# Rotary tables copied on chip, late constants, and products by pieces of tokens, in the start-up of a hybrid decoder block

## The chip, the cores and the metric

The kernel runs on all 8 cores of one Trainium2 chip (two dies: cores 0 to 3 and 4 to 7). The time is the device time of the slowest core, in microseconds (us). Most executions agree within 0.3%. Some fall in a slow state, in which the cores of a die run at a lower granted clock and the time is several per cent longer. Ratios of two kernels are computed as the mean time of one kernel's fast runs over that of the other's fast runs of the same rounds on the same chip, so they are not quite the ratio of the medians that are quoted.

In the profile PE is TensorE's matmuls, PEld its weight loads, DVE is VectorE, ACT ScalarE, POOL GpSimd and SP SyncE. SPq is SyncE as the issuer of transfers.

## The reference, cut to what matters

The whole program is one decoder block: a gated short convolution and a latent attention side by side, then a feed-forward network. The change touches only the first stage, in which every core computes the key/value latents of all 4096 tokens.

```python
def rope_tables(positions, dtype):
    inv_freq = ROPE_THETA ** (-jnp.arange(0, QK_ROPE_DIM, 2, dtype=jnp.float32) / QK_ROPE_DIM)
    ang = positions.astype(jnp.float32)[..., None] * inv_freq          # (B, S, 32)
    cos = jnp.cos(ang)[:, :, None, :].astype(dtype)
    sin = jnp.sin(ang)[:, :, None, :].astype(dtype)
    return cos, sin

# ... in reference():
u = rmsnorm(h, ln1_g[l])
z = u @ w_in[l]
zb, zc, zv, q_lat, kv_lat, k_rope, gates = jnp.split(z, IN_SPLIT_IDX, axis=-1)
# ... kv_lat (512 columns) and k_rope (64 columns) are needed for all tokens;
#     k_rope gets the rotary embedding from cos and sin
```

## The kernel before

Tokens come in 16 groups of two blocks of 128 tokens (so 256 columns in a product). For each group TensorE multiplies 16 slices of the input weights (128 rows each) with the tokens, in five column tiles m = 0 to 4: 80 products of 128x256. A slice of weights is loaded as float32 and scaled by ScalarE with the norm's gain into bfloat16 before it can be used; group 0's products follow those 16 scalings one by one.

Three loads:

- the *tokens* of a group, loaded and converted to bfloat16 by transfers that GpSimd issues (`xpiece`), two of 512 KB for a group;
- the *own blocks*, one float32 copy of 1 MB for each group with tokens of this core (`oload`), issued by SyncE. The first three belong to groups 2, 3 and 4;
- the *sine tables*: ScalarE computes sine and cosine on 128 partitions, and SyncE writes them to DRAM and reads them back into four copies of 32 partitions (`sine`, `csload`).

```python
    def xpiece(g, h, k, n, behind=()):
        x, Tx = xtile(g)
        r = PAIRS[g][h] * 128
        dma(POOL, x[:, h, k:k + n, :].rearrange("p k n -> p (k n)"), xg[r:r + 128, k * 128:(k + n) * 128],
            "x%d%d%d" % (slot[g], h, k), reads=behind, writes=Tx[h][k // 4:(k + n) // 4])

    def xload(g, behind=()):
        for h in range(g in OWN_G, 2):
            xpiece(g, h, 0, 16, behind)
        F1.pos["ld%d" % g] = 1

    def oload(i, behind=()):
        dma(SP, xo_[i % 3].rearrange("p k n -> p (k n)"), xg[i * 512:i * 512 + 128, :], "xw%d" % (i % 3), reads=behind,
            writes=[Txo[i % 3]])
        F1.mark("old", i)

    def wscale(k):
        act(wkv[:, k, :], wst[k % 8], AF.Copy, [Twst[k % 8], Tcst], [Twk[k]], scale=C("g1", k))
        if k < 8:
            wload(k + 8)
        F1.mark("w", k)

    def sine(which):
        q, Tq = angle[which]
        dst, Tdst = ((tS, TtS), (tC, TtC))[which]
        act(dst, q, AF.Sin, [Tq], [Tdst])
        x = 1 - which
        dma(SP, cs_d[128 * x:128 * x + 128, :], dst, "csw%d" % x, reads=[Tdst], writes=[Tcsd[x]])
        if which == 0:
            return
        csload(0, 1)
        oload(0)
        dma(SP, xhb.rearrange("p a b -> p (a b)"), xh, "xh", writes=[Txhb])
    # [cut: csload(q0, q1), four reads of cs_d into CS for the tables q0 to q1]

    for k in range(16):
        if k in (5, 9):
            f_w.units.append(Unit(lambda k=k: sine(k // 9), 0.0, pos=-9.0, ok=lambda k=k: F1.at("ang") >= k // 9))
        f_w.units.append(Unit(lambda k=k: wscale(k), 0.0, pos=-9.0))
    # [cut]
    for k in range(16):
        def first(k=k):
            for m in (0, 2, 4):
                latents(0, m, k, k + 1)
        f_l.units.append(Unit(first, 0.33, need=[Twk[k], ...], ...))
    for m in (1, 3):
        def second(m=m):
            latents(0, m)
            lpost(0, m)
        f_l.units.append(Unit(second, 1.75, ...))
    # [cut]
            if i > 0:
                f_d.units.append(Unit(lambda i=i: oload(i), 0.0, pos=-9.0,
                                      ok=lambda i=i: at("ld%d" % (i + 1)) > 0 and at("own") >= i - 3 and at("cast") >= i - 3))
            if i == 1:
                f_d.units.append(Unit(lambda: csload(1, 4), 0.0, pos=-9.0, ok=lambda: at("ld3") > 0))
        if g == 1:
            f_g.units.append(Unit(lambda: xload(1, [Twst[5]]), 0.0, pos=-9.0, ok=lambda: at("w") >= 8))
        # [cut]
        for h in range(2):
            f_a.units.append(Unit(lambda g=g, h=h: squares(g, h), 0.0, pos=g - 2.0,
                                  ok=lambda g=g, h=h: (at("ld%d" % g) > 0 if h or g not in OWN_G
                                                       else at("cast") >= OWN_G.index(g))
                                  and at("xst") >= g - 2 and at("xs") >= 2 * g + h - 2))
```

The `Unit`s are not chosen at run time. A small list scheduler merges the streams while the program is built, with estimated costs, and each engine then executes its own list strictly in order. An instruction whose data are late holds up everything behind it on its engine, also what has nothing to do with it. `squares` on ScalarE (the sum for the norm of a group) needs the group's tokens. `at("ld1") > 0` in its condition says only that the load has been *issued*.

## Time and profile before

| | before |
|---|---|
| median (4 fast runs, 2601.16 to 2608.04) | 2604.19 us |
| slowest core of the profiled run | core 4, 2604.2 us |
| TensorE busy | 2527.1 us, 97% |
| TensorE waiting in the first 206 us, slowest core | 38.0 us |
| the same, mean of 8 cores (sum of its list of waits) | 39.4 us |

The page of the kernel before: busy time of each engine with its share and number of instructions, the chain of work that ended last by engine, and the group of ScalarE's table loads (busy time, mean ns).

```profile
PE 2527.1 (97%) x18238; PEld 1639.3 (63%) x18338; DVE 1503.8 (58%) x3051; ACT 1033.2 (40%) x2044; POOL 184.6 (7%) x321
...
PE 91%; DMA 4%; DVE 2%; issue 1%; ACT 1%; SPq 0%; DVEq 0%; ACTq 0%; POOL 0%; POOLq 0%
...
L521 ACT ACT_TABLE_LOAD x5 | 6.4, 1283 | 27.6 <-DVE arena L528 14.2
```

TensorE is the bottleneck, so only its own idle time can be gained. The list of TensorE's waits in the first 206 us of the kernel before (waited for; us in total, times, longest) shows how much that is:

```profile
PE ps L514 <- ACT arena L521: 33.5, 13, 13.2
PE ps L514 <- DMA arena<-xg: 3.4, 1, 3.4
PE ps L514 <- DVE arena L532: 1.1, 1, 1.1
```

The timeline of TensorE of the kernel before (start, duration, group, and in brackets the idle time ahead of it with what ended it) shows where the tokens come in:

```profile
36.16 3.57 PE L514 MATMUL ps<-arena 128*128 128x256 bf16 x16 [2.49 <-ACT arena L521]
41.51 6.44 PE L514 MATMUL ps<-arena 128*128 128x256 bf16 x41 [1.78 <-ACT arena L521]
51.34 13.67 PE L514 MATMUL ps<-arena 128*128 128x256 bf16 x110 [3.39 <-DMA arena<-xg]
```

Group 0's products end at 47.95 (41.51 + 6.44). Group 1's begin at 51.34, when its tokens have landed.

The timeline of the transfers that SyncE issues in the kernel before (start of the issue, time it took, transfer):

```profile
22.77 0.65 SPq L548 DMA_DIRECT2D cs_d<-arena  x1
26.57 3.84 SPq L548 DMA_DIRECT2D arena<-wkvin  x3
35.37 0.33 SPq L548 DMA_DIRECT2D cs_d<-arena  x1
39.03 4.29 SPq L548 DMA_DIRECT2D arena<-cs_d  x4
43.37 0.45 SPq L548 DMA_DIRECT2D arena<-xg  x1
...
44.53 0.71 SPq L548 DMA_DIRECT2D arena<-xg  x1
45.28 2.48 SPq L548 DMA_DIRECT2D arena<-cs_d  x4
47.80 0.44 SPq L548 DMA_DIRECT2D arena<-xg  x1
```

### The profile page before, as it was taken

The numbers are of one execution on the slowest core, as the hardware profiler recorded it, in microseconds if no ns is written. First come the engines' busy times: TensorE is split into PE (matmuls) and PEld (weight loads), VectorE is DVE, ScalarE is ACT, GpSimd is POOL, SyncE is SP. The second block draws the span as 40 slices with busy tenths as digits, with TensorE's granted clock in tenths as the row PEclk, the third lists the DMA queues.
The fourth block names the chain that finished last, engine by engine and source line by source line (L and its number), as shares of the span: only waits on it lengthen the run. The fifth ranks groups of instructions, "written<-read, shape, count | busy, mean of one in ns | idle before, by whom it ended". The sixth has DMA issues, their size and how long they took to land.

```text
span 2604.2 us, 51904 instructions; the slowest of 8 cores (2585.0 to 2604.2 us)
## 1 busy us (share of the span) xinstructions
PE 2527.1 (97%) x18238; PEld 1639.3 (63%) x18338; DVE 1503.8 (58%) x3051; ACT 1033.2 (40%) x2044; POOL 184.6 (7%) x321
## 2 busy tenths in 40 slices
PE   4999999999999999999999999999999999999996
PEld 3886666666666666666666666666466556645652
DVE  3882787787787877842121122477457637745752
ACT  5883788888888888731111123200000000000000
POOL 1010000000000000000000000010101110110010
PEclk9999999999999999999999999999999999999998
DMA  9674121102020121434444474443454454345455
GB/s 211 164 131 75 19 38 26 35 19 51 18 43 18 39 38 27 120 69 74 77 74 74 77 188 94 72 75 66 74 87 74 67 85 77 68 73 87 74 93 134
DMA packets 64636, 195.69 MB, mean 75 GB/s; under 512 B 7232, under 2 KB 8512, under 8 KB 63296
## 3 DMA queue, kind: packets, MB, share of 16 engines
q0 software_dynamic: 45648, 144.33, 33.6%
q1 hardware_dynamic: 18736, 48.03, 5.8%
q8 instruction: 154, 2.52, 0.4%
q14 instruction: 98, 0.80, 0.1%
HBM read 320.30 MB, written 15.83 MB: 129 GB/s over the span
## 4 chain that ended last, share of the span: by engine, by line
PE 91%; DMA 4%; DVE 2%; issue 1%; ACT 1%; SPq 0%; DVEq 0%; ACTq 0%; POOL 0%; POOLq 0%
PE ps L514 91%; DMA outT<-arena 2%; DVE arena L532 1%; DMA arena<-wkvin 1%; DVE arena L528 1%; ACT arena L521 1%; DMA arena<-xg 0%; SPq L548 0%; DVEq L200 0%; DVE arena L541 0%; DVE arena L538 0%; ACTq L200 0%; SPq L200 0%; DVE arena L545 0%; POOL arena L548 0%
## 5 line engine op out<-in xcount | busy, mean ns | idle before, releaser
L514 PE MATMUL ps<-arena 128*128 128x390 bf16 (+9 forms) x18238 | 2527.1, 299 | 61.1 <-ACT arena L521 37.4
L514 PEld LDWEIGHTS ps<-arena 128*128 128x128 bf16 x18338 | 1639.3, 98 | 948.4 <-issue 89.5
L532 DVE TENSOR_TENSOR arena<-ps,arena 128x390 f32<-128x390 f32 (+6 forms) x744 | 374.4, 510 | 814.1 <-PE ps L514 720.9
L532 DVE TENSOR_TENSOR arena<-arena 128x130 bf16<-128x130 bf16 (+18 forms) x1522 | 663.6, 474 | 228.8 <-ACT arena L521 201.4
L521 ACT ACTIVATE arena<-ps,arena 128x260 bf16<-128x260 f32 (+7 forms) x992 | 519.8, 547 | 418.6 <-PE ps L514 363.2
L521 ACT ACTIVATE arena<-arena 128x390 bf16<-128x390 f32 (+14 forms) x412 | 269.3, 678 | 913.7 <-DVE arena L528 800.3
L528 DVE SCALAR_TENSOR_TENSOR arena<-arena 128x1024 f32<-128x1024 f32 (+9 forms) x499 | 371.7, 761 | 37.1 <-ACT arena L521 13.1
L521 ACT ACTIVATE arena<-ps 128x512 bf16<-128x512 f32 (+11 forms) x635 | 320.3, 525 | 114.8 <-PE ps L514 108.8
L548 POOL DMA_DIRECT2D arena<-wall x286 | 167.3, 585 | 2243.9 <-PE ps L514 2184.9
L541 DVE TENSOR_SCALAR arena<-arena 128x1024 f32<-128x1024 f32 (+1 forms) x90 | 72.3, 803 | 0.0
L528 DVE SCALAR_TENSOR_TENSOR arena<-ps,arena 128x256 bf16<-128x256 f32 (+1 forms) x80 | 33.2, 463 | 6.4 <-ACT arena L521 4.2
L548 POOL DMA_DIRECT2D arena<-xg x30 | 16.6, 569 | 139.8 <-PE ps L514 63.3
L521 ACT ACT_TABLE_LOAD x5 | 6.4, 1283 | 27.6 <-DVE arena L528 14.2
L538 DVE TENSOR_SCALAR arena<-arena 128x390 f32<-128x390 f32 (+2 forms) x29 | 16.2, 560 | 1.7 <-DMA arena<-cst 0.3
L532 DVE TENSOR_TENSOR arena<-arena,ps 128x390 bf16<-128x390 f32 (+1 forms) x24 | 12.3, 511 | 1.6 <-PE ps L514 1.3
L545 DVE COPY arena<-ps 128x2 f32<-128x2 f32 (+1 forms) x32 | 7.0, 219 | 2.4 <-PE ps L514 1.9
L545 DVE CAST arena<-arena 128x1028 f32<-128x1028 int32 (+1 forms) x5 | 3.5, 708 | 3.7 <-DMA arena<-posg 3.3
L545 DVE COPY arena<-arena 128x6 f32<-128x6 f32 (+1 forms) x24 | 3.8, 160 | 0.7
L772 DVE MEMSET arena<- 128x128 bf16 x1 | 0.2, 165 | 1.2 <-PEq L425 1.2
L965 DVE MEMSET arena<- 64x512 bf16 x1 | 0.5, 485 | 0.1
L548 POOL DMA_DIRECT2D arena<-cst x1 | 0.5, 537 | 0.0
L425 POOL MEMSET const-float32-0.0<- 128x1 f32 x1 | 0.1, 99 | 0.5 <-issue 0.5
(3 smaller groups left out, 0.3 us busy)
## 6 DMA issues: line engine op xcount, KB each, us to landing
arena<-wall POOLq DMA_DIRECT2D x182, 512.0 KB, 5.3
arena<-wall POOLq DMA_DIRECT2D x64, 352.0 KB, 5.0
arena<-xg POOLq DMA_DIRECT2D x22, 512.0 KB, 9.4
arena<-xo SPq DMA_DIRECT2D x16, 520.0 KB, 21.0
arena<-xg SPq DMA_DIRECT2D x8, 1024.0 KB, 6.1
arena<-wall POOLq DMA_DIRECT2D x32, 256.0 KB, 3.7
outT<-arena SPq DMA_DIRECT2D x32, 256.0 KB, 2.8
arena<-wkvin SPq DMA_DIRECT2D x16, 320.0 KB, 15.1
```

Of the source, the lines that this page charges most:

```text
L425: nc = bass.Bass("TRN2", target_bir_lowering=False)
L514: S.add(PE, lambda e: e.matmul(out, lhsT=lhsT, rhs=rhs, start=start, stop=stop), reads, writes, cost=max(width(rhs) / 2400.0, 0.055) + 0.003)
L521: S.add(ACT, lambda e: e.activation(out=out, in_=in_, func=func, **kw), reads, writes, cost=c)
L528: S.add(DVE, lambda e: e.scalar_tensor_tensor(out=out, in0=in0, scalar=scalar, in1=in1, op0=op0, op1=op1), reads, writes, cost=dcost(out, ...
L532: S.add(DVE, lambda e: e.tensor_tensor(out=out, in0=in0, in1=in1, op=op), reads, writes, cost=dcost(out, in0, in1) + held)
L538: S.add(DVE, lambda e: e.tensor_scalar(out=out, in0=in0, scalar1=s1, scalar2=None, op0=op0), reads, writes, cost=c)
L541: S.add(DVE, lambda e: e.tensor_scalar(out=out, in0=in0, scalar1=s1, scalar2=s2, op0=op0, op1=op1), reads, writes, cost=c)
L545: S.add(DVE, lambda e: e.tensor_copy(out=out, in_=in_), reads, writes, cost=dcost(out, in_))
L548: S.add(eng, lambda e: e.dma_start(out=out, in_=in_), reads=reads, writes=writes, chan=chan, cost=in_.shape[0] * width(in_) * esz(in_.dtyp ...
L772: S.add(DVE, lambda e: e.memset(ones, 1.0), writes=[Tones], cost=0.2)
L965: f_t.units.append(Unit(lambda: S.add(DVE, lambda e: e.memset(sqkr[64:128, :, :], 0.0), writes=Tsqkr), 0.0, pos=-8.5))
```

## The change

The intent: the sine tables no longer go through DRAM. ScalarE computes each of the eight pieces of 32 partitions straight into its place, and VectorE makes the second copy. The weight slices shrink from 640 to 576 columns, and VectorE makes the missing 64 by two copies of 32. Constants that are needed later, the mask and the halos load later. Group 0 does all five products of a slice as soon as the slice is scaled, and group 1's tokens come in eight pieces of 128 KB, with its products following the pieces. The core of the diff (moved constants, renamed regions and the later uses of the constants are cut):

```diff
+EARLY = (0, 1)
 ...
-    wkvin = din("wkvin", [128, 16 * 640])
+    wkvin = din("wkvin", [128, 16 * 576])
 ...
     def xload(g, behind=()):
-        for h in range(g in OWN_G, 2):
-            xpiece(g, h, 0, 16, behind)
+        n = 4 if g in EARLY else 16
+        for k in range(0, 16, n):
+            for h in range(g in OWN_G, 2):
+                xpiece(g, h, k, n, behind)
 ...
-        act(wkv[:, k, :], wst[k % 8], AF.Copy, [Twst[k % 8], Tcst], [Twk[k]], scale=C("g1", k))
+        act(wkv[:, k, 0:576], wst[k % 8], AF.Copy, [Twst[k % 8], Tcst], [Twk[k]], scale=C("g1", k))
         if k < 8:
             wload(k + 8)
+        for o, i in ((576, 544), (608, 512)):
+            cp(wkv[:, k, o:o + 32], wkv[:, k, i:i + 32], [Twk[k]], [Twk[k]])
 ...
-    def sine(which):                  # [cut: with the writes to DRAM, csload(0, 1), oload(0), halos]
+    def sines(q):
+        o = slice(1028 * q, 1028 * q + 1028)
+        for r, which in ((0, 1), (2, 0)):
+            v, Tv = angle[which]
+            act(CS[32 * r:32 * r + 32, o], v[32 * q:32 * q + 32, :], AF.Sin, [Tv], [TCSk[q]])
+            cp(CS[32 * r + 32:32 * r + 64, o], CS[32 * r:32 * r + 32, o], [TCSk[q]], [TCSk[q]])
+        F1.mark("tab", q)
+
+    def late_loads():
         dma(SP, xhb.rearrange("p a b -> p (a b)"), xh, "xh", writes=[Txhb])
-    def csload(q0, q1):               # [cut]
+        dma(SP, cst[:, CO["bgate"]:], cstd[:, CO["bgate"]:NC_CONST - 528], "cst2", writes=[Tcst2])
 ...
+    for q in range(4):
+        f_t.units.append(Unit(lambda q=q: sines(q), 0.0, pos=-9.0))
     for k in range(16):
-        if k in (5, 9):
-            f_w.units.append(Unit(lambda k=k: sine(k // 9), ...))
         f_w.units.append(Unit(lambda k=k: wscale(k), 0.0, pos=-9.0))
     for k in range(16):
         def first(k=k):
-            for m in (0, 2, 4):
+            for m in range(5):
                 latents(0, m, k, k + 1)
 ...
+            if i == 0:
+                f_d.units.append(Unit(lambda: oload(0, [Twst[7]]), 0.0, pos=-9.0, ok=lambda: at("ld1") > 0))
 ...
+        if 0 < g and g in EARLY:
+            for k in range(0, 16, 4):
+                def lat4(g=g, k=k):
+                    for m in range(5):
+                        latents(g, m, k, k + 4)
+                    ...
```

## The prediction

> **What bounds it now.** The engine table gives TensorE 97% of the span (2527.1 of 2604.2 us); the chain of waits is 91% TensorE. The change touches only the start-up (key latents, first 206 us). There TensorE's list of waits shows 38 us idle: 33.5 behind ScalarE, 3.4 behind loads of tokens, 1.1 behind VectorE; 13.2 of it lies before the first product. So 38 us (1.5%) is the ceiling, of which 10 to 13 cannot go.
>
> Why it waits (timeline, 0 to 70 us): the DMA share is 1.0 from 10 to 30 us and from 40 to 70. The SyncE queue stands at the first sine table's write to DRAM until 22.8 us; the last three weight loads come behind it (issued at 26.6 to 30.4). ScalarE's 6th scaling waits 3.0 us for weights, then ScalarE works without a gap from 29.2 to 38.2. Group 0's products end at 48.0; group 1's wait for tokens until 51.3.
>
> **Removed or moved.** Table writes (2 x 514 KB) and reads (4 x 128.5, 4 x 385.5 KB): 3.1 MB. Weights 320 to 288 KB each: 0.5 MB. Late constants, mask and halos, 0.7 MB, go later. Together 4.3 MB; at the 220 to 260 GB/s of 10 to 30 us an estimated 17 to 19 us of transfers, about half of it ahead of group 1's tokens. By DMA alone these could land near 42 us, 9 earlier.
>
> **Added.** ScalarE: 8 sines on 32 partitions instead of 2 on 128; width sets the cost, so about 1.05 us each: +6.3 us. The 16 scalings lose 0.05 us each (-0.8). In the new order, the logarithm and exponential of group 0's norm fall between sines. The trace has table loads at 10.7 and 38.2 us (1.28 us each), the second just before the first logarithm; so two more: +2.6 us. (The Trainium skill, "ScalarE: Activation LUTs", section "What ACT_TABLE_LOAD costs", states about 1283 ns plus a drain; the load agrees with this trace.) So ScalarE gets 8 us more while TensorE already waits for it. VectorE: 32 copies of 32 columns (estimate 0.1 us each) and 8 of 1028 (about 0.7): 9 us, in idle time, but between scaling and product.
>
> **On the critical path.** My estimate: the 8th weight lands near 26 us instead of 29; then ScalarE works without a gap until the 16th scaling near 46 (before: 42.8). Group 0 ends at 47 (48.0), but with all five products of each slice done and group 1's tokens there, group 1 follows at once instead of at 51.3: about 4 us, and some us of later waits. Of 15 us that DMA alone would free, ScalarE takes back about half. After 206 us TensorE's order is the same.
>
> **Prediction: 2597 us (-0.3%), range 2586 to 2606.** Faster by over 2%: 0.01; within 2%: 0.98; slower by over 2%: 0.01.
>
> **To check.** TensorE's idle in the first 206 us: from 38 to about 31. Table loads: 7 instead of 5. ScalarE without a gap over 1 us from about 26 to 46; 16th scaling between 42 and 48. Group 1's first product 4 to 6 us earlier, tokens no longer its last wait. DMA share below 1.0 at 40 to 70 us. The stretch after 206 us unchanged within 3 us.
>
> **What would make it wrong.** If ScalarE keeps up (fewer table loads, shorter sines), the gain rises to 12 to 15 us. If VectorE's copies hold the products, or table loads fall into later groups too, it goes to zero. The slowest of eight cores is timed; their spans differ by 19 us, so a few us can drown.

## More of the kernel before

The timeline of GpSimd of the kernel before, with the tokens of groups 1 and 2 (four transfers):

```profile
39.66 2.12 POOL L548 DMA_DIRECT2D arena<-xg  x4 [32.60 <-DMA arena<-wkvin]
```

SyncE's list is in order. The second table write waits for the sine until 35.37, the four table reads wait for that write until 39.03, and the three own-block loads of 1 MB (`arena<-xg`) come only at 43.37, 44.53 and 47.80. Group 1's tokens are issued at 39.66 to about 41. So the table traffic, slow as it is, also keeps 3 MB behind the tokens.

## The result, and the profile after

| | before | after |
|---|---|---|
| median of 4 fast runs | 2604.19 us | 2607.72 us (2606.99 to 2608.21) |
| ratio of fast runs, 95% interval | | 1.0013, 0.9995 to 1.0030: the same |
| TensorE waiting in the first 206 us, slowest core | 38.0 us | 43.2 us |
| the same, mean of 8 cores | 39.4 us | 41.2 us |
| products begun by 60 us, mean of 8 cores (sum over windows) | 149 | 88 |
| products begun by 190 us, mean of 8 cores (sum over windows) | 1330 | 1289 |

The changed kernel is no faster, and the prediction of a small gain was wrong. The whole span is a poor ruler for a few us, because the slowest of eight cores is timed and their spans differ by up to 19 us. So I use a second one, called the *lead*: the products that TensorE has begun by a moment (from the view by windows, mean of the eight cores), minus those of the kernel before at that moment, times 0.1058 us, since between 170 and 190 us the kernel before does 189 products in 20 us. It is an estimate. For the changed kernel it is -0.6 us at 50 us, -6.4 at 60 and -4.4 at 190. (A product that lies across the border of two windows is counted in both, in both kernels; one window from 0 to 190 us has 1317 and 1278 products, and -4.2 us.) A count of the weight loads in place of the products gives the same within 0.2 us, so records missing from the trace do not make it. The waits alone grow by less than that, by 1.8 us in the mean of the cores: the products also took longer each (by 190 us TensorE was busy for 0.116 us a product, against 0.115 before). A third ruler is a ScalarE table load near 1140 us, called the *marker*: its mean over the cores is 1138.6 us before and 1143.1 after, 4.5 us later. So the loss arises before 60 us, and most of it stays.

The page of the changed kernel, the lines that answer to those of before:

```profile
PE 2533.8 (97%) x18338; PEld 1639.5 (63%) x18338; DVE 1511.3 (58%) x3091; ACT 1039.8 (40%) x2052; POOL 188.3 (7%) x327
...
PE 90%; DMA 4%; DVE 2%; issue 1%; ACT 1%; SPq 0%; POOL 0%; DVEq 0%; ACTq 0%; POOLq 0%
...
L524 ACT ACT_TABLE_LOAD x7 | 9.0, 1283 | 27.2 <-DVE arena L531 14.2
```

The two extra table loads are there, as predicted. (The trace of before lacks 100 records of matmuls, as its own weight loads show: 18338 against 18238. The difference of busy PE time is therefore not a finding.) The list of TensorE's waits of the changed kernel, same stretch:

```profile
PE ps L517 <- DVE arena L548: 40.2, 14, 13.8
PE ps L517 <- DVE arena L535: 3.0, 3, 1.3
```

The name has changed from ScalarE to VectorE's copies (L548 in the changed kernel is the copy, where L548 of before was a transfer). This is not yet a cause: the two copies of 32 columns follow each scaling, so they are merely the last link. What holds *them* has to be looked up. TensorE's timeline of the changed kernel:

```profile
48.21 1.23 PE L517 MATMUL ps<-arena 128*128 128x256 bf16 x5 [3.92 <-DVE arena L548]
50.09 1.22 PE L517 MATMUL ps<-arena 128*128 128x256 bf16 x5 [0.66 <-DVE arena L548]
60.56 14.60 PE L517 MATMUL ps<-arena 128*128 128x256 bf16 x110 [9.25 <-DVE arena L548]
```

After the 15th slice TensorE stands still for 9.25 us, until 60.56. The other cores show the same wait, of 6.05 to 9.25 us. It is the *last slice of group 0* that is late. ScalarE's timeline of the changed kernel tells why:

```profile
34.85 7.29 ACT L524 ACTIVATE arena<-arena 32x1028 f32<-32x1028 f32 x7 [2.54 <-DVE arena L541]
42.16 1.28 ACT L524 ACT_TABLE_LOAD   x1
...
44.35 1.28 ACT L524 ACT_TABLE_LOAD   x1
45.65 3.74 ACT L524 ACTIVATE arena<-arena 32x1028 f32<-32x1028 f32 x4
49.30 0.36 ACT L524 ACTIVATE arena<-ps 128x256 f32<-128x256 f32 x1
56.01 7.98 ACT L524 ACTIVATE arena<-arena 128x2048 bf16<-128x2048 bf16 x7 [6.35 <-DMA arena<-xg]
```

ScalarE finishes at 49.66 and then waits 6.35 us for `xg`, group 1's tokens, because the square of group 1 (128x2048) stands in its list *ahead of* the 16th scaling. From 56.01 it does that square and one sine, and then the scaling, which ends at 59.8; VectorE's two copies follow. The tokens are the root, and their transfers stand in these lines. First GpSimd's timeline of the changed kernel (eight pieces of group 1, then two transfers of group 2), then SyncE's:

```profile
33.15 6.32 POOL L551 DMA_DIRECT2D arena<-xg  x10 [26.89 <-DMA arena<-wkvin]
```

```profile
34.15 2.48 SPq L551 DMA_DIRECT2D arena<-xg  x3
```

SyncE issues all three own-block loads from 34.15 to 36.63, among the pieces of group 1. The view of transfers from 30 to 60 us (transfer, issuing queue, number, KB each, median us from issue to landing) shows what that costs. In the changed kernel:

```profile
arena<-xg SPq DMA_DIRECT2D x3, 1024.0 KB, 13.0
arena<-xg POOLq DMA_DIRECT2D x8, 128.0 KB, 17.5
arena<-xg POOLq DMA_DIRECT2D x2, 512.0 KB, 21.6
```

A piece of 128 KB takes 17.5 us to land. In the kernel before, the four whole blocks of 512 KB took 13.7 us in the same view, and the two of group 1 alone 8.9 us.

The view by windows (first the length, then busy time of PE, PEld, DVE, ACT and POOL with the number of instructions, the granted clock, the DMA share and GB/s), changed kernel, slowest core:

```profile
40.00:50.00 10.00, 4.54 (x19) 2.05 (x17) 3.89 (x12) 9.40 (x12) 0.00 (x0) 1.00 1.04 302
50.00:60.00 10.00, 1.22 (x5) 0.58 (x5) 1.85 (x4) 3.91 (x4) 0.00 (x0) 1.00 1.03 164
60.00:70.00 10.00, 9.44 (x63) 7.39 (x64) 4.50 (x11) 9.77 (x10) 0.00 (x0) 1.00 0.02 4
```

The transfers keep the DMA engines full until 60 us and are then idle. The bytes did become fewer; but the burst that remains falls just where the tokens have to land.

### The profile page after: what moved, and what is told of

Same layout as the page of the kernel before. It is cut to its first block, busy times and chain, and to the rows that moved or that the text cites. A ratio compares the mean times of both kernels' runs of the same rounds, so it can differ in the third digit from the quotient of the medians.

```text
span 2606.5 us, 52111 instructions; the slowest of 8 cores (2592.8 to 2606.5 us)
## 1 busy us (share of the span) xinstructions
PE 2533.8 (97%) x18338; PEld 1639.5 (63%) x18338; DVE 1511.3 (58%) x3091; ACT 1039.8 (40%) x2052; POOL 188.3 (7%) x327
## 4 chain that ended last, share of the span: by engine, by line
PE 90%; DMA 4%; DVE 2%; issue 1%; ACT 1%; SPq 0%; POOL 0%; DVEq 0%; ACTq 0%; POOLq 0%
PE ps L517 90%; DMA outT<-arena 2%; DVE arena L535 1%; ACT arena L524 1%; DMA arena<-wkvin 1%; DMA arena<-xg 1%; DVE arena L531 1%; SPq L551 0%; POOL arena L551 0%; DVEq L200 0%; DVE arena L548 0%; DVE arena L544 0%; DVE arena L541 0%; ACTq L200 0%; SPq L200 0%
## 5 line engine op out<-in xcount | busy, mean ns | idle before, releaser
L517 PE MATMUL ps<-arena 128*128 128x390 bf16 (+9 forms) x18338 | 2533.8, 300 | 61.3 <-DVE arena L548 40.2
L535 DVE TENSOR_TENSOR arena<-arena 128x130 bf16<-128x130 bf16 (+19 forms) x1522 | 663.2, 474 | 216.5 <-ACT arena L524 190.0
L524 ACT ACTIVATE arena<-arena 128x390 bf16<-128x390 f32 (+14 forms) x418 | 275.2, 681 | 926.7 <-DVE arena L531 798.6
L524 ACT ACTIVATE arena<-ps 128x512 bf16<-128x512 f32 (+12 forms) x635 | 320.1, 525 | 101.8 <-PE ps L517 95.9
L548 DVE COPY arena<-arena 128x32 bf16<-128x32 bf16 (+3 forms) x64 | 14.7, 232 | 22.4 <-ACT arena L524 20.7
L524 ACT ACT_TABLE_LOAD x7 | 9.0, 1283 | 27.2 <-DVE arena L531 14.2
L541 DVE TENSOR_SCALAR arena<-arena 128x390 f32<-128x390 f32 (+2 forms) x29 | 16.2, 560 | 1.3 <-DVE arena L548 0.2
L548 DVE COPY arena<-ps 128x2 f32<-128x2 f32 (+1 forms) x32 | 7.0, 220 | 3.7 <-PE ps L517 3.5
L548 DVE CAST arena<-arena 128x1028 f32<-128x1028 int32 (+1 forms) x5 | 3.5, 696 | 4.1 <-DMA arena<-posg 4.1
```

The source lines that it names most:

```text
L517: S.add(PE, lambda e: e.matmul(out, lhsT=lhsT, rhs=rhs, start=start, stop=stop), reads, writes, cost=max(width(rhs) / 2400.0, 0.055) + 0.003)
L524: S.add(ACT, lambda e: e.activation(out=out, in_=in_, func=func, **kw), reads, writes, cost=c)
L535: S.add(DVE, lambda e: e.tensor_tensor(out=out, in0=in0, in1=in1, op=op), reads, writes, cost=dcost(out, in0, in1) + held)
L541: S.add(DVE, lambda e: e.tensor_scalar(out=out, in0=in0, scalar1=s1, scalar2=None, op0=op0), reads, writes, cost=c)
L548: S.add(DVE, lambda e: e.tensor_copy(out=out, in_=in_), reads, writes, cost=dcost(out, in_))
```

## The experiments

My theory, from the two traces: the removed table traffic had also been a gate for the own-block loads. Without it they run beside group 1's tokens and delay them, and ScalarE's fixed order turns the late tokens into a stall of group 0's last scaling. The rivals: the order of ScalarE alone is to blame (the square ahead of the scaling); P, the eight small pieces load worse than two whole blocks; ScalarE's own added work (eight sines, two table loads); and later V, any lead is given back by VectorE between 80 and 110 us. Expectations that speak of the marker mean the table load near 1140 us.

All kernels below gave correct results. "Lead" is against the kernel before. Its times in the four batches had medians of 2604.5, 2605.4, 2605.9 and 2605.0 us (slow runs counted in).

| run | in short | median us | ratio (95%) | lead at 60 | lead at 190 | marker |
|---|---|---|---|---|---|---|
| (changed kernel) | | 2607.72 | 1.0013 (0.9995, 1.0030) | -6.4 | -4.4 | 1143.1 |
| e14 | changed kernel again | 2606.69 | 1.0008 (0.9994, 1.0021) | -6.2 | -4.4 | 1143.2 |
| e1 | own loads held | 2603.75 | 0.9981 (0.9922, 1.0040) | -2.4 | -0.8 | 1139.8 |
| e2 | square behind the scaling | 2605.51 | 0.9992 (0.9942, 1.0043) | -0.9 | -4.3 | 1143.0 |
| e3 | both | 2606.22 | 0.9989 (0.9938, 1.0041) | -0.7 | -2.6 | 1140.2 |
| e4 | e2 and whole tokens | 2632.0 | 1.0055 (0.9986, 1.0123) | -0.6 | -4.9 | 1144.0 |
| e5 | held, no extra table loads | 2603.39 | 0.9992 (0.9974, 1.0010) | 1.9 | 1.7 | 1139.6 |
| e7 | e5, sines behind all scalings | 2601.39 | 0.9988 (0.9972, 1.0004) | 2.4 | 1.3 | 1138.1 |
| e8 | e5, two whole sines | 2598.76 | 0.9974 (0.9956, 0.9992) | 2.9 | 3.9 | 1134.9 |
| e10 | e8, tokens earlier | 2596.84 | 0.9967 (0.9951, 0.9983) | 2.9 | 3.7 | 1134.5 |
| e12 | e10, sines last | 2608.7 | 1.0016 (1.0003, 1.0029) | 2.6 | -5.9 | 1144.7 |
| e13 | *before*, own loads early | 2612.63 | 1.0031 (1.0015, 1.0047) | -5.8 | -9.5 | 1148.4 |
| e15 | e8 without the hold | 2606.38 | 1.0000 (0.9979, 1.0022) | 1.0 | -2.5 | 1141.2 |

e4's seven runs were 2606.81, 2607.88, three at 2630 to 2632 us, which its ratio counts as fast, and two near 3000 and above. The kernel before also had one run of 2633.83 among the fast ones of that batch (e1 to e4). It widens those four intervals and lowers the ratios; without it the means would give about 1.000 for e1 and 1.001 for e2 and e3. So the times of this batch decide nothing, and the traces have to. e5, e8, e12, e13, e15 had one slow run each, e1 two and e3 one, which the ratios leave out.

### e1_hold_own: the own-block loads wait for group 1's tokens

```diff
-oload(0, [Twst[7]])
+oload(0, [xtile(1)[1][h][3] for h in range(2)])     # the last pieces of group 1's tokens
```

> Changed kernel, with one edit: the three own-block loads of the SyncE queue (1 MB each) wait until the last pieces of group 1's tokens have landed. The order of ScalarE up to the 16th scaling is the same. Marker of the start-up: the time at which ScalarE loads its table near 1140 us (mean of eight cores 1138.6 before, 1143.1 after the change). Theory C (contention: the own-block loads, freed from behind the table transfers, take half of the bandwidth of group 1's tokens): the tokens land near 46 us instead of 56, the square of group 1 starts near 46, the 16th scaling ends near 50, TensorE resumes near 51 instead of 60.6 on the slowest core; marker 1134 to 1137, whole time 6 to 9 us below the changed kernel. Rival O (order on ScalarE alone: the square stands ahead of the 16th scaling; when the tokens land is given by their own 8 small transfers): tokens still after 53 us, gain under 2 us.

Measured: 2603.75 us, ratio 0.9981, an interval too wide to decide by itself. The trace decides. SyncE's timeline of e1, then TensorE's, then the view of transfers from 30 to 60 us:

```profile
43.92 1.66 SPq L551 DMA_DIRECT2D arena<-xg  x3
```

```profile
52.35 12.50 PE L517 MATMUL ps<-arena 128*128 128x256 bf16 x95 [2.78 <-DVE arena L548]
```

```profile
arena<-xg SPq DMA_DIRECT2D x3, 1024.0 KB, 11.3
arena<-xg POOLq DMA_DIRECT2D x8, 128.0 KB, 4.9
```

The own loads start at 43.92, and since they wait for nothing but the last pieces, this is when the tokens have landed: 12 us earlier than in the changed kernel. A piece takes 4.9 us instead of 17.5. The wait of 9.25 us before group 0's last slice shrinks to 2.78 us, on all eight cores. The lead goes from -6.4 to -2.4 at 60 us and from -4.4 to -0.8 at 190, by one changed dependency. ScalarE's operations come in the same order in both traces up to 54 us, past the 16th scaling, and TensorE's up to 60; after that the scheduler's new order differs, so the 4.0 us at 60 are the contention and what follows from it, and the 3.6 at 190 also hold a change of order. It is less than I had expected: the marker was to fall to 1134 to 1137 and is 1139.8.

### e2_square_late: the square of group 1 only after the 16th scaling

```diff
                                   and at("xst") >= g - 2 and at("xs") >= 2 * g + h - 2
+                                  and (g == 0 or at("w") >= 15)
```

> Changed kernel, with one edit: the squares of group 1 may be placed on ScalarE only after the 16th scaling. Own-block loads as in the changed kernel. Theory C: tokens of group 1 still land near 55 us; group 0's last slice is done near 52 instead of 61, group 1's slices follow from about 54, so the marker falls by 3 to 6 us (1137 to 1140) but not to what holding the own-block loads gives. Rival O: this alone gives the whole of what was expected of the change, a marker near 1134. If neither the order nor the late tokens matter (VectorE's copies are the limit): no change, within 1 us of 1143.

Measured: 2605.51 us, ratio 0.9992. ScalarE's timeline of e2, and TensorE's:

```profile
54.84 2.99 ACT L524 ACTIVATE arena<-arena 128x2048 bf16<-128x2048 bf16 x2 [2.61 <-DMA arena<-xg]
```

```profile
51.85 12.07 PE L517 MATMUL ps<-arena 128*128 128x256 bf16 x89 [0.91 <-DVE arena L548]
```

TensorE now has its last slice at 51.85 instead of 60.56, but the tokens still land only at about 54.8, and the lead, -0.9 at 60 us, is back at -4.3 at 190. The order of ScalarE decides *which* work the late tokens stall. Moving the stall elsewhere does not remove it. That the order alone is to blame falls with this run, but my own forecast missed too: the marker was to fall to 1137 to 1140, and is 1143.0. Why it is given back in full between 60 and 90 us (-0.6 at 70, -5.0 at 90) this run does not show.

### e3_both: e1 and e2 together

```diff
+ the edits of e1 and of e2
```

> Both edits: own-block loads held behind group 1's tokens, and group 1's squares after the 16th scaling. Theory C: tokens near 46 us, 16th scaling ends near 48, TensorE goes on without a gap over 2 us from about 49; marker 1132 to 1136, whole time 7 to 11 us below the changed kernel and 3 to 8 below the kernel before. Rival O: the same as with the squares late alone, within 1.5 us.

Measured: 2606.22 us, ratio 0.9989, lead +0.9 at 70 us but -2.6 at 190, no better than e1 alone. The tokens land at 43.6, and the 16th scaling is nevertheless done only at about 50, just ahead of TensorE's resumption at 50.79. The marker, 1140.2, misses the 1132 to 1136 that I had expected. Even with no wait for tokens, ScalarE is later than the 46 that the prediction gave it. The loss from 90 to 110 us (three waits of 1.09, 0.52 and 2.46 us behind VectorE) is a matter of the new static order that I could not settle.

### e4_whole_tokens: e2 with group 1's tokens in two whole blocks

```diff
+ the edit of e2
-EARLY = (0, 1)
+EARLY = (0,)
```

> Group 1's tokens loaded whole again (two transfers of 1 MB, products by output block as before), with group 1's squares after the 16th scaling, to be read against the run that has only the squares late. Theory C: the first half of the tokens lands a few us earlier, the second still after 52 us, because the own-block loads still run beside them; marker equal or up to 4 us later than with pieces. Rival P (the eight small transfers are slow in themselves: 0.6 us of GpSimd each, 2 KB rows): both halves land before 48 us, marker at least 3 us earlier than with pieces.

Measured: 2606.81 us at best, ratio 1.0055 with a wide interval; lead at 190 us -4.9 and marker 1144.0, against -4.3 and 1143.0 of e2. The view of transfers on core 4, kept to group 1's tokens: the two whole blocks of e4, then the eight pieces of e2.

```profile
arena<-xg POOLq DMA_DIRECT2D x2, 512.0 KB, 10.9
arena<-xg POOLq DMA_DIRECT2D x8, 128.0 KB, 17.5
```

On this core the second whole block landed at 46.8 us, and the last piece of e2 at 55.5; on the eight cores it is 43.8 to 48.0 against 51.7 to 56.1. So rival P was right about the landing: beside free own loads, the pieces are what makes the tokens 6.5 to 8.8 us later. The blocks are issued at 32.0 and 32.9, ahead of the own loads (33.0 to 33.9). The pieces are issued one after another until 37.5, so most of them come behind the own loads, and they also land behind them. Holding the own loads (e1) or not splitting the tokens: each brings the tokens in early. So in the changed kernel the late landing takes both, the early own loads and the pieces.

P was wrong about the time: the marker was to be at least 3 us earlier, and is 1.0 later. On the slowest core (3) TensorE takes up its last slice at 51.14 and goes on with group 1, but then waits 4.08 us behind VectorE until 65.17, and VectorE had itself waited 4.30 us for ScalarE until 62.43. With the tokens in time, ScalarE's list is the next limit, as in e3.

### e5_sines_before_log: hold, late square, and no extra table loads

Here only the second and third own loads are held (the first is free). The sum for the first norm, which needs a logarithm, waits for all sines, so ScalarE changes its tables no more often than before. Two conditions put the conversion of own blocks behind the squares.

```diff
-oload(i)
+oload(i, [xtile(1)[1][h][3] for h in range(2)] if i == 1 else ())
+ the edit of e2
 # conversion of an own block:
-at("old") >= i and done()
+at("old") >= i and done() and at("sq") >= 3 and (i == 0 or at("lout") >= 0)
 # statistics of a group:
-at("xs") >= 2 * g + 1 and at("kys") >= g - 3 and ...
+at("tab") >= 3 and at("xs") >= 2 * g + 1 and at("kys") >= g - 3 and ...
```

> Base of this and the next three runs: only the second and third own-block loads wait for group 1's tokens; squares of group 1 after the 16th scaling; casts of own blocks after the squares of group 1 (the second one also after group 0's results); the logarithm of group 0's norm after the last sine, so that two table loads fall away (5 in all instead of 7). Theory W (with the contention gone, ScalarE's own work holds TensorE: 6 sines more and two table loads more): the 16th scaling ends 2 to 3 us earlier than in the run with both edits (50 us), and TensorE is about 25 products ahead of it at 60 us. Theory V (what is won before 70 us is given back from 80 to 110 us, where VectorE is over 95% busy): the marker near 1140 us still does not fall below 1137 (mean of eight cores: 1138.6 before, 1140.2 with both edits). If the two table loads do not matter: same as both edits within 1 us.

Measured: 2603.39 us, ratio 0.9992 (0.9974, 1.0010), five table loads. TensorE is back at 47.05 instead of 50.79 (e3), and the lead is +1.9 at 60 us and +1.7 at 190: for the first time it stays positive. (The marker, 1139.6, is also what theory V had forecast for this run; e8 tells the two apart.) ScalarE's timeline of e5:

```profile
33.30 17.15 ACT L524 ACTIVATE arena<-arena 32x1028 f32<-32x1028 f32 x16 [2.54 <-DVE arena L541]
```

There are now 17 us of ScalarE work without a gap, in which the sines and scalings alternate. Ahead of it still stands a wait of 2.54 us for VectorE's clamp of the angles (L541). It is the same in the changed kernel (see its ScalarE timeline above). VectorE's in-order list has the copies of each scaled slice between the steps of the angles, so the angles come later. I had not foreseen this wait.

### e7_weights_first: e5 with all sines behind the 16th scaling

```diff
-f_t.units.append(Unit(lambda q=q: sines(q), 0.0, pos=-9.0))
+f_t.units.append(Unit(lambda q=q: sines(q), 0.0, pos=-9.0, ok=lambda: at("w") >= 15))
```

> As the base, but all eight sines only after the 16th scaling; ScalarE's work is the same, its order is not. Theory W: the 16th scaling ends near 39 us, group 0's products near 41, group 1's start when its tokens land (44 to 48 us); TensorE is 30 to 60 products ahead of the base at 55 us, but loses them again while ScalarE does the sines, so the marker is that of the base within 1.5 us. If only the order of the scalings counted, the marker would be 5 us or more below the base.

Measured: 2601.39 us, ratio 0.9988 (0.9972, 1.0004). The 16th scaling comes at about 38.8, and the lead at 50 us is +7.0; at 70 it is -1.6. TensorE's timeline of e7 shows the debt:

```profile
62.54 1.01 PE L517 MATMUL ps<-arena 128*128 128x256 bf16 x4 [7.49 <-ACT arena L524]
```

The lead at 190 us is +1.3, no more than e5's +1.7. When the sines come later, TensorE waits for ScalarE later. Order alone buys nothing here. This fits the theory that the total work counts which ScalarE has to do before TensorE can run freely.

### e8_whole_sines: e5 with two sines on 128 partitions

ScalarE computes the two tables at full partition width, in place, as in the kernel before, and VectorE makes all sixteen copies of 32 partitions.

```diff
     def sines(q):
         o = slice(1028 * q, 1028 * q + 1028)
-        for r, which in ((0, 1), (2, 0)):
+        if q == 0:
+            for which in (0, 1):
+                v, Tv = angle[which]
+                act(v, v, AF.Sin, [Tv], [Tv])
+        for r, which in ((0, 1), (1, 1), (2, 0), (3, 0)):
             v, Tv = angle[which]
-            act(CS[32 * r:32 * r + 32, o], v[32 * q:32 * q + 32, :], AF.Sin, [Tv], [TCSk[q]])
-            cp(CS[32 * r + 32:32 * r + 64, o], CS[32 * r:32 * r + 32, o], [TCSk[q]], [TCSk[q]])
+            cp(CS[32 * r:32 * r + 32, o], v[32 * q:32 * q + 32, :], [Tv], [TCSk[q]])
```

> As the base, but two sines of 128 partitions, in place, and sixteen copies by VectorE instead of eight sines of 32 partitions and eight copies: takes 5.6 us away from ScalarE and gives as much to VectorE before 55 us, where it has idle time. Theory W: 16th scaling ends near 41 us, TensorE 40 to 70 products ahead of the base at 60 us, marker at least 3 us below the base. Theory V: the lead at 70 us shrinks to less than half of itself by 110 us.

Measured: 2598.76 us, ratio 0.9974 (0.9956, 0.9992): faster than the kernel before, by a quarter of a per cent. The durations behind it, from the groups of ScalarE by shape, 0 to 75 us (number, busy time, mean ns): first the kernel before, with two sines of 128 partitions, then the changed kernel with eight of 32.

```profile
L521 ACT ACTIVATE arena<-arena 128x1028 f32<-128x1028 f32 x2 | 2.1, 1052 | 0.0
```

```profile
L524 ACT ACTIVATE arena<-arena 32x1028 f32<-32x1028 f32 x8 | 8.5, 1057 | 2.7 <-DVE arena L541 2.5
```

A quarter of the partitions takes the same time, as the prediction had it. TensorE's timeline of e8:

```profile
44.52 10.31 PE L517 MATMUL ps<-arena 128*128 128x256 bf16 x93 [0.27 <-DVE arena L548]
```

Group 1 follows group 0 without a stop, from 44.5 us, as the prediction had wanted of the changed kernel. The lead is +4.1 at 50 us, dips to +1.9 at 70 (TensorE waits 3.53 us behind VectorE until 59.51), and is +5.0 at 110 and +3.9 at 190. Theory V, that VectorE gives the lead back between 80 and 110, falls: it grows there, although VectorE has eight more copies to do.

### e10_tokens_early: e8 with group 1's tokens released three weight slices sooner

```diff
-xload(1, [Twst[5]])
+xload(1, [Twst[2]])
```

> As the run with whole sines, and group 1's tokens are released by the 11th weight slice instead of the 14th, which closes a gap of 4 to 5 us in which the DMA engines had little to do (30 to 37 us). Contention theory C with W: tokens land 3 to 4 us earlier and TensorE, which then waits for them, is 25 to 35 products ahead of the run before at 60 us; marker 1 to 4 us lower. If VectorE is the limit from 80 us on (V): marker within 1 us of the run with whole sines.

Measured: 2596.84 us, ratio 0.9967 (0.9951, 0.9983), lead +3.7 at 190 us, the same as e8. The 25 to 35 products that I had expected did not come: e8 has no wait for group 1's tokens left, and where the tokens are there when ScalarE and TensorE get to them, sooner is no better. (An equal marker was also what V forecast; since e8 left nothing to gain, this run does not test V.) e8 and e10 differ by 1.9 us of median with the same lead, which I take as noise. e10 is the best version found. It beats both kernels, still by far less than 2%.

### e11_no_hold and e15_no_hold_again: e8 with the own loads free

```diff
-oload(i, [xtile(1)[1][h][3] for h in range(2)] if i == 1 else ())
+oload(i)
```

This asks what the contention costs when ScalarE's load is the light one. The first attempt:

> The run with whole sines, but with all three own-block loads as free as in the changed kernel (they start when the last weight slice has landed, about 33 us). ScalarE's order is the same up to the square of group 2. Theory C (contention): the tokens of group 1 land at 52 to 56 us again instead of near 46, TensorE, which in the run with whole sines goes on at 44.5 us, waits for them 5 us or more in all between 44 and 56 us, and is 40 products or more behind the run with whole sines at 55 us; at 190 us it has lost 20 products or more of that run's lead. If the contention mattered only through ScalarE's order (the square ahead of the 16th scaling): within 10 products of the run with whole sines at 55 and 190 us.

It fell in the slow state (profiled run 2958.24 us at granted clocks of 0.85 to 0.95, against 0.99 and more in fast runs), so its trace says nothing. Its one fast run of five took 2604.9 us. The identical kernel again:

> The same kernel as the run that fell into the slow state: whole sines, own-block loads free. Theory C (contention): tokens of group 1 land at 52 to 56 us, TensorE waits 5 us or more in all between 44 and 56 us, is 40 products or more behind the run with the loads held at 60 us, and keeps a loss of 20 products or more at 190 us; whole time 2600 to 2605 us. If the contention mattered only through ScalarE's order: within 10 products at 60 and 190 us, and about 2598.5 us.

Measured: 2606.38 us, ratio 1.0000 (0.9979, 1.0022). The lead is -2.5 us at 190, against +3.9 of e8. The traces of e8 and e15 hold the same instructions in the same order on every engine, so no change of static order is mixed in: 6.4 us go to the contention. They show late: at 60 us e15 is only 1.9 us, or 18 products, behind e8, where I had expected 40 or more. TensorE's timeline of e15, then ScalarE's:

```profile
52.88 9.92 PE L517 MATMUL ps<-arena 128*128 128x256 bf16 x68 [4.42 <-DMA arena<-xg]
```

```profile
55.30 5.61 ACT L524 ACTIVATE arena<-arena 128x2048 bf16<-128x2048 bf16 x4 [8.17 <-DMA arena<-xg]
```

Here the square stands behind the scalings, so the wait bears its own name: TensorE waits 4.42 us and ScalarE 8.17 us for `xg`. The own loads are issued at 33.93 and the pieces take 17.6 us to land, against 8.4 in e8.

### e12_sines_last: e10 with the two sines behind the 16th scaling

```diff
+ in e10: sines(q) only after at("w") >= 15, as in e7
```

> Towards a better version: whole sines after the 16th scaling, tokens of group 1 released early, second and third own-block loads held. Theory W: 16th scaling ends near 38 us, group 1 starts near 41 to 43, TensorE 10 to 25 products ahead of the best run so far at 50 us; whole time 2594 to 2598 us, 7 to 10 below the kernel before. If what is left is a wait later than 55 us (group 0's norm, released late), the lead is gone by 70 us and the time is that of the best run so far within 2 us.

Measured: 2608.7 us, ratio 1.0016 (1.0003, 1.0029): a miss. The lead is +8.5 us at 50 and +1.5 at 90, and then falls to -4.8 at 110. TensorE waits 7.29 us behind ScalarE at 57.4, 3.40 us behind VectorE at 61.8 and 4.58 us behind VectorE at 99. The first two are e7's debt again. What makes the last one I could not settle. It confirms that an early lead is no gain by itself.

### e13_before_own_early: the kernel *before*, with its own-block loads put ahead of the table write

If the gate is the point, then opening it in the kernel before must hurt it in the same way, with none of the change's other parts.

```diff
     def sine(which):
         ...
+        if which == 1:
+            for i in range(3):
+                oload(i, [Twst[5]])
         dma(SP, cs_d[128 * x:128 * x + 128, :], dst, ...)
         ...
         csload(0, 1)
-        oload(0)
 ...
-            if i > 0:
+            if i > 2:
                 f_d.units.append(Unit(lambda i=i: oload(i), ...))
```

> The kernel before, with the three own-block loads put on the SyncE queue ahead of the second table write, released by the same weight slice as group 1's tokens (about 39 us): the suspected cost of the change added to the kernel before, without anything else of the change. Theory C: group 1's tokens land at 55 to 60 us instead of 51.3, its first product comes 3 us or more later than 51.3, TensorE's waiting before 60 us grows by 3 us or more. If contention of these loads is not the cause, the first product of group 1 stays within 1.5 us of 51.3.

Measured: 2612.63 us, ratio 1.0031 (1.0015, 1.0047): slower, with an interval that excludes 1. SyncE's timeline of e13, then TensorE's:

```profile
39.76 1.28 SPq L548 DMA_DIRECT2D arena<-xg  x3
```

```profile
61.35 5.07 PE L514 MATMUL ps<-arena 128*128 128x256 bf16 x23 [10.34 <-DMA arena<-xg]
```

Group 1's first product waits 10.34 us for tokens instead of 3.39 (7.2 to 11.5 us on the eight cores; 0.5 to 4.4 on seven cores of the kernel before, and none on the eighth), and the lead is -5.8 us at 60. The same loads, moved ahead by about 4 to 7 us, cost nearly what the changed kernel loses at 60 us (6.4), without any of its other parts. Here the tokens are whole blocks, and two of the three own loads are issued ahead of them. Two reservations. On the core shown, group 0's products were already 1.9 us later than in the kernel before, ahead of these loads. And the table reads also come later here, which may be part of the further fall to -9.5 at 190 us.

### e14_changed_again: the changed kernel, unedited

```diff
  (no edit)
```

> The changed kernel again, beside these runs on the same chip, unedited: 2605 to 2610 us, 1 to 5 us above the kernel before; if the first result was chance, below it.

Measured: 2606.69 us, ratio 1.0008 (0.9994, 1.0021), lead -6.2 at 60 and -4.4 at 190, marker 1143.2. In a later batch the leads at 60 and 190 us and the marker repeat within 0.2 us (at 70 us the lead differs by 0.7), so by this one repetition differences of 2 us in the lead can be read.

## Why the prediction was wrong

**The step that failed** is this one: "with all five products of each slice done and group 1's tokens there, group 1 follows at once instead of at 51.3". The tokens were not there. It rests on the sentence "By DMA alone these could land near 42 us, 9 earlier", which counted the bytes that go away and let everything else stay where it was. But the removed transfers stood in SyncE's in-order queue ahead of three loads of 1 MB. Taking them out moved those loads from 43.4 to 47.8 us up to 34.2 to 36.6 us, beside the tokens. The tokens landed at 56.0 instead of 51.3. Held back, they land at 43.9 (e1). That is close to the 42 of the prediction, but its sum had no hold in it, so this does not confirm the sum. The pieces, which the change itself brought in, have their part in it: whole blocks, issued ahead of the own loads, land by 48.0 even beside them (e4). The kernel before, given the same early own loads, loses the same way (e13), and with a light ScalarE the hold alone is worth 6.4 us (e8 against e15). It is not the only limit: with the tokens in time and ScalarE's work left as it is, the lead at 190 us is still -2.6 (e3) and -4.9 (e4).

**What made it worse.** ScalarE's static order has group 1's square ahead of the last scaling, so late tokens of group 1 stalled *group 0* by 6.05 to 9.25 us. I had the static order of the changed kernel before me and checked the sines and table loads in it, but not which of its instructions depend on a load that could be late. Without the contention this order costs much less: 2.78 us in e1.

**The other terms:**

- *ScalarE's added work: right in size.* Predicted +6.3 us for the sines, +2.6 us for two table loads. Measured 8.5 - 2.1 = 6.4 us, and two loads of 1.283 us. The runs confirm that it matters: without the two table loads and with the holds the lead is +1.7 us (e5, which changes other conditions too), without the long sines as well +3.9 (e8).
- *VectorE's copies: 9 us, as an estimate.* Measured 5.3 + 5.5 = 10.8 us on the slowest core (173 ns for 32 columns, 688 ns for 1028).
- *The 8th weight near 26 us instead of 29: right in the gain.* The scaling that uses it begins at 27.6 us in the mean of the cores, against 30.3 before.
- *ScalarE without a gap from 26 to 46, 16th scaling at 42 to 48: wrong.* It waited 2.54 us for VectorE's angles, then 6.35 us for tokens. Even with tokens in time the 16th scaling came at about 50 (e3), at 46 without the extra table loads (e5), and at 40 with two whole sines (e8).
- *TensorE's idle from 38 to 31: wrong.* 43.2 us on the slowest core; in the mean of the cores 41.2 against 39.4.
- *Group 1's first product 4 to 6 us earlier: wrong.* Group 0's last slice started at 60.56, so group 1's first product came about 10 us later than before.
- *DMA share below 1.0 from 40 to 70: wrong* until 60 us (1.04 and 1.03), and 0.02 after. The bytes were saved, but after the moment where they mattered.
- *The stretch after 206 us unchanged: right* as far as the rulers tell. The lead at 190 us is -4.4 and the marker near 1140 us is 4.5 us later.
- *Within 2%: right.* The range, 2586 to 2606, missed the median by 1.7 us, and the direction was wrong.

The prediction named two ways in which the gain could go to zero: VectorE's copies holding the products, and more table loads. The list of waits seems to show the first (40.2 us behind the copies), but this is a name, not a cause: e1 cut the wait ahead of group 0's last slice from 9.25 to 2.78 us without touching a copy. What I did not name was a load that becomes *earlier*.

The mechanism that I predicted does exist. With the own loads held, the square late, no extra table loads and whole sines, group 1 follows group 0 at once (e8), and the time is 2598.76 us, or 2596.84 with e10, about what I had predicted for the change as it stands.

**What stays open.** Why the early leads of e2, e3 and e12 are given back between 60 and 110 us; the scheduler makes a new order for every edit, and I found waits behind ScalarE and VectorE there but not their common cause. How much the later constants and halos are worth: no run has them alone. What whole blocks of tokens alone would do to the changed kernel: e4 has the late square as well. The pieces show no gain of their own (e2 against e4: 0.6 us of lead, too little to read).

## What to carry to other kernels

A slow transfer in an in-order queue is also a gate: before removing it, list what stands behind it, when that will start instead, and what it will then run beside. A load that is split into pieces is issued over a longer time, and its late pieces come behind whatever another queue issues meanwhile (landed at 55.5 us with pieces, e2, and at 46.8 whole, e4). When a static in-order list puts a data-dependent instruction ahead of unrelated work, a late load stalls that unrelated work, and the list of waits names only the last link; follow it back to the engine that waited for something outside. And splitting an operation over fewer partitions did not make it cheaper on ScalarE (1057 ns on 32 partitions, 1052 ns on 128); here its time went by width.

## What the Trainium skill lacked or had wrong

- "DMA: Bandwidth & Descriptors", section "Issuing engines are not separate DMA queues", says that transfers issued by different engines end up on the same 16 DMA engines and interleave. The traces agree. What that section lacks is a measured cost for a load that others wait for: pieces of 128 KB landed in 4.9 us (median) with no own loads beside them (e1) and in 17.5 us with 3 MB of another queue beside them (changed kernel); whole blocks issued ahead of the same 3 MB landed in 10.9 us (e4, core 4).
- "ScalarE: Activation LUTs", section "What ACT_TABLE_LOAD costs", gives about 1283 ns for the load, and the trace has 1283 ns. It adds a drain of about 1380 ns, 2.66 us in all. The changed kernel's load starts at 42.16 as the work ahead of it ends (34.85 + 7.29 = 42.14), and the next instruction starts at 43.46, 1.3 us later.
- The same section gives 186 ns + 0.833 ns per column for an instruction with immediate operands on 128 partitions, worked out 1042 ns for 1028 columns; measured 1052 ns. It gives no measurement on fewer partitions. These runs do: 1057 ns for 32 partitions.
- "TensorE: Matmul & The Clock Gate", Part 1, says that an array that has been idle runs at 1.2 GHz and a busy one at 2.4 GHz. The isolated slices of group 0 took 1.22 to 1.23 us for five products of 256 columns (0.246 us each, with the tail of the last), against 0.106 us each in steady flow. So a product in the start-up costs about twice, as the page would have it; these runs do not separate the clock from weight loads that nothing covers in a slice on its own. The granted clock in the records does not show it: those slices read 1.23 us both where the windows give 1.00 (changed kernel, 40 to 50 us) and where they give 0.50 (e1, 40 to 50 us). The page has a caveat on the events of this gate; it could name the granted clock too.
